# Feature-major sample columns, S5's a and final states transposed on TensorE instead of moved by element, and B loaded in two transfers

## The chip, the cores and the metric

The kernel runs on one core of a Trainium2 chip. The metric is the device time of one execution in microseconds; the figure for a kernel is the median of its runs. TensorE (PE) multiplies matrices, VectorE (DVE), ScalarE (ACT) and GpSimd (POOL) work element by element, and SyncE (SP) does nothing but issue transfers. ACT issues transfers too, on a queue of its own.

## What is computed

One inference step of a decoder of two layers, for a prompt of 2048 tokens and, beside it, 8 sample sequences of one token each. Both use the same weights.

```
for each layer l:
    proj = rms_norm(x) @ w_in[l]          # 1024 -> 3336 columns, cut into 15 groups
    A  retention on r_q, r_k, r_v         B  mLSTM on m_q, m_k, m_v, m_i, m_f
    C  S5 (complex diagonal SSM) on s_u   D  attention of a_q into 256 memory tokens
    mix = [A | B | C | D], each times its SiLU gate
    x   = x + mix @ w_out[l]
outputs: rms_norm(x) of prompt and sample, and each group's final states
```

The S5 group has 16 channel groups of 64 complex states: a (16x64, real and imaginary), B (16x64x16), C (16x16x64). Its final prompt states are outputs of 16x64 each. The state of the 8 samples is read from inputs, advanced by one token and written back.

## The kernel before

The prompt is cut into 4 units of 512 tokens a layer. A unit runs through the column groups of w_in in a fixed order (`ORDER`): m_v, s_u, then the four quarters of w_out for the unit before, m_k, m_q, m_o, a_q, r_k, r_v, r_q, s_g, a_g, m_g, r_g; in unit 1 of layer 0 the four quarters of w_out come after a_q. Weights are kept as two float32r halves. The first time that a group's weights are used they are loaded raw, split on ACT, DVE and POOL and stored to DRAM (`ws`); later units load both halves from there (`w<-ws`, 256 KB a transfer, on SP). Each product is three matmuls, high x high, high x low, low x high.

Seven groups (`FEAT`: m_k, m_q, a_q, s_g, a_g, s_u, r_q) are computed feature-major, features on partitions and tokens in columns; the others token-major. In unit 1 of each layer (the sample unit) the 8 sample tokens are computed as well. For a feature-major group they are 8 more columns behind the 512 of the prompt, and each of its two halves of 128 features is done in two pieces of 260 columns. The second piece ends in the 8 sample columns. Line 480 copies them out of PSUM, and line 481 stores them to the DRAM table `sproj[l]` (8 rows of 3336 columns), which lies sample-major: 128 partitions x 8 columns become 1024 runs of one element. That is 14 stores a layer. For token-major groups `sample_group` (from line 1538) multiplies the 8 samples by themselves and stores rows of 256 columns.

Work beside the main groups is written as generators that are stepped after every main step (`sides`, `step_sides`). `s5_pre` builds the S5 tables of a layer: layer 0's from the start, layer 1's, slowed by a factor, from unit 2 of layer 0 on. Its first step (lines 1121 to 1129) loads a with four transfers by element (partition = state, column = channel group, so 64x16 single elements each), dt, and B with four transfers of 1024 runs of 64 B (real over imaginary, and imaginary over real). `s_core` is the S5 of a unit: it loads tables by quarters (`s_tables`: sWi, sCS, sTW), runs a scan on DVE, carries the state in `xprev` (128 x 16), sends Y through DRAM to turn it and, in the last unit, stores `xprev` with two transfers of 1024 elements (lines 1390 to 1392). `sample_layer` starts after the sample unit's r_g, slowed as well; it reads `sproj` back in many layouts and ends in stores to `smix`, which the last unit's w_out groups need. Its S5 part, `sample_s5`, loads u, feature on partition, with eight transfers of 32 x 8 elements (lines 1784 and 1785).

`dma` issues on SP, `dmaa` on ACT. Small tiles come from rotating pools: `sm` has 17 buffers, `t1` 3, `t2` 12, and `bank()` gives one of four PSUM banks `ps`; a new tile waits until its buffer's last reader is done. The tile framework plans the order of the instructions of each engine when the program is built, from a simulated timeline; within an engine, and within a queue, the planned order is kept. Helpers record one line for all their callers: `mm` 181, `tr` 185, `act` 188, `dma` 191, `dmaa` 194.

Of the kernel before, what the change touches and what calls it, by code (L numbers as in the profile page):

```python
# [22 lines left out]
SG = 16  # L23
# [5 lines left out]
D_IN = 3336  # L29
# [4 lines left out]
NB = 8  # L34
# [80 lines left out]
def AP(t, off, ap):  # L115
    return bass.AP(tensor=t.tensor, offset=t.offset + off, ap=[list(x) for x in ap])


class Builder:
# [93 lines left out]
    def setup(self):  # L213
        nc, I, cp = self.nc, self.I, self.cp
        c = lambda n, s, dt=F32: cp.tile(s, dt, name=n, tag=n)
        self.ident = c("ident", [128, 128])
        self.dma(self.ident, I["c_ident"])
        self.wstream()
        self.mem_load()
        self.wload(0)  # L220
        self.hnl = self.hn_load(0, 0)
        next(self.hnl)
        self.wload(1)
        self.maskb = c("maskb", [128, 512], BF16)
        self.identb = c("identb", [128, 128], BF16)
        mt = self.t2([128, 512])
        self.dma(mt, I["c_mask"])
        nc.vector.tensor_copy(self.maskb, mt)
        nc.vector.tensor_copy(self.identb, self.ident)
        self.Dt = c("Dt", [128, 2, 2, 128])  # L230
        self.dma(self.Dt, I["c_D"])
        self.vd = c("vd", [128, H])
        self.dma(self.vd, I["c_vd"])
        self.ropes = c("ropes", [128, 2, 16])
        self.dma(self.ropes, I["c_ropes"])
        self.smc = c("smc", [128, 4])
        self.dma(self.smc, I["c_sm"])
        self.e127 = c("e127", [128, 1])
        self.dma(self.e127, I["c_e127"])
        self.s32 = c("s32", [128, 32])  # L240
        self.dma(self.s32, I["c_s32"])
        self.s8 = c("s8", [128, 8])
        self.dma(self.s8, I["c_s8"])
        st = self.t2([128, H])
        self.dma(st, I["c_sel"])
        self.sel = c("sel", [128, H], F32R)
        nc.vector.tensor_copy(self.sel, st)
        zero = self.t2([128, 320])
        nc.vector.memset(zero, 0.0)
        self.ones = c("ones", [128, 1])  # L250
        nc.vector.memset(self.ones, 1.0)

        self.hT = [cp.tile([128, 8, UT + NB], F32R, name=f"hT{i}", tag=f"hT{i}") for i in range(2)]
        self.Sr = [c(f"Sr{i}", [128, 2, 128]) for i in range(3)]
        self.Cm = [c(f"Cm{i}", [128, 2, 130]) for i in range(3)]
        for t in self.Sr + self.Cm:
            nc.vector.memset(t, 0.0)
        self.mprev = c("mprev", [4, 8])
        self.hS = [c(f"hS{i}", [128, 8, 40], F32R) for i in range(2)]
        for i in range(2):  # L260
            nc.vector.tensor_copy(self.hS[i].rearrange("p a b -> p (a b)"), zero)

        T = self.T
        self.xd = [self.dram([T, D], f"xd{i}") for i in range(self.depth)]
        self.xsd = [self.dram([NB, D], f"xsd{i}") for i in range(self.depth)]
        self.sproj = [self.dram([NB, D_IN], f"sproj{i}") for i in range(self.depth)]
        self.smix = [self.dram([NB, D], f"smix{i}") for i in range(self.depth)]
        self.stab = []
        self.memd = []
        for l in range(self.depth):  # L270
            self.stab.append(dict(
                Wi=self.dram([128, SG, 128], f"Wi{l}"), TW=self.dram([128, 3, 1024], f"TW{l}"),
                CS=self.dram([128, 2, SG, 128], f"CS{l}"), Kd=self.dram([32, 16, 112], f"Kd{l}"), ab=self.dram([128, 3, SG], f"ab{l}"),
                C1=self.dram([128, SG, SC], f"C1{l}")))
            self.memd.append((self.dram([128, 2, MEM], f"mk{l}"), self.dram([128, 2, GW], f"mv{l}")))
# [173 lines left out]
    def group(self, i):  # L449
        kind, l, b, g = self.wseq[i]  # L450
        if i == 0:
            self.wsplit(0, 0)
            self.wsplit(0, 1)
        hi, lo, _ = self.wspl[i]
        if kind == "mem":
            self.mem_group(l, b, hi, lo)
            self.advance(i, 0)
            self.advance(i, 1)
            yield
        elif kind == "out":  # L460
            if self.sample_in_unit(kind, l, b):
                while not self.smix_done[l]:
                    self.step_sides()
                self.sample_group(i, l, g, hi, lo, kind)
            yield from self.group_out(i, l, b, g, hi, lo)
        elif g in FEAT:
            if g == "r_q":
                for m in range(2):
                    self.u["rq", m] = self.g4([128, 2, UT], n="rqt")
                    self.dmaa(self.u["rq", m], self.I["c_rq"][b, m])  # L470
            smp = self.sample_in_unit(kind, l, b)
            pieces = [(0, 260), (260, 520)] if smp else [(0, UT)]
            for m in range(2):
                for c0, c1 in pieces:
                    ps = self.feat_bank(m, hi, lo, slice(c0, c1))
                    c2 = min(c1, UT)
                    self.evac_f(l, b, g, m, ps[:, :c2 - c0], slice(c0, c2))
                    if c1 > UT:
                        o = self.sm([128, 16])[:, :NB]
                        self.nc.vector.tensor_copy(o, ps[:, c2 - c0:c1 - c0])  # L480
                        self.dma(AP(self.sproj[l], COL[g] + 128 * m, [[1, 128], [D_IN, NB]]), o)
                    if (c0, m) == (0, 0):
                        self.advance(i, 0)
                    if c1 >= UT and m == 1:
                        self.advance(i, 1)
                    yield
        else:
            if g == "m_v":
                jobs = [[t] for t in range(4)]
            else:  # L490
                jobs = [[0, 1], [2, 3]]
            n = 264 if g == "m_v" else 256
            for m, ts in enumerate(jobs):
                sls = [slice(t * 128, (t + 1) * 128) for t in ts]
                ps = self.tok_bank(sls, n, hi, lo, self.hslice)
                self.evac(l, b, g, m, ps)
                if m in (0, len(jobs) - 1):
                    self.advance(i, min(m, 1))
                if g == "r_g":
                    nxt = self.next_unit(l, b)  # L500
                    if nxt:
                        self.hn_T(2 * m)
                        self.hn_T(2 * m + 1)
                yield
        if kind == "in" and g not in FEAT and self.sample_in_unit(kind, l, b):
            self.sample_group(i, l, g, hi, lo, kind)
# [605 lines left out]
    def s5_pre(self, l):  # L1112
# [5 lines left out]
        packA = self.t2([128, 512], n="packA")  # L1118
        packC = self.t2([128, 2, SG, SC], n="packC")
        ar, ai, dt = S(), S(), S()  # L1120
        for h in range(2):
            self.dma(ar[64 * h:64 * h + 64], I["s5_a_re"][l].rearrange("g p -> p g"))
            self.dma(ai[64 * h:64 * h + 64], I["s5_a_im"][l].rearrange("g p -> p g"))
        self.dma(dt, AP(I["s5_log_dt"][l], 0, [[0, 128], [1, SG]]))
        Bst = P1([2, SG, SC], "Bst")
        for h in range(2):
            for w in range(2):
                src = I["s5_b_re" if h == w else "s5_b_im"][l]
                self.dma(Bst[64 * h:64 * h + 64, w], src.rearrange("g p c -> p g c"))
        yield  # L1130
        yield
        self.pexp(dt, SG)
        mag, th, cs, sn, k, tmp, thl = S(), S(), S(), S(), S(), S(), S()
        v.tensor_tensor(mag, ar, dt, OP.mult)
# [186 lines left out]
    def s_core(self, u, l, b):  # L1321
# [66 lines left out]
        yield  # L1388
        yield
        if b == self.NU - 1:  # L1390
            for h, on in enumerate(("s5re_p", "s5im_p")):
                self.dma(self.O[on][l, 0].rearrange("g p -> p g"), self.xprev[64 * h:64 * h + 64])
        gl = self.g4([128, 2, UT], n="gl")
        gh_, gl_ = [self.g4([128, 2, UT], F32R, n="gls") for _ in range(2)]
        for gh in range(2):
# [142 lines left out]
    def sample_group(self, i, l, g, hi, lo, kind):  # L1538
# [16 lines left out]
        else:  # L1555
# [5 lines left out]
            if g == 3:  # L1561
                if l + 1 < self.depth:
                    self.dma(self.xsd[l], self.xrow)
                    self.sample_hn(l + 1, self.xrow)
                else:
                    w = self.bcrow(self.I["final_norm_w"])
                    self.rms_rows([self.xrow], w[:NB], NB)
                    self.dma(self.O["y_sample"].rearrange("b o d -> (b o) d"), self.xrow)

    def s_load(self, t, l, name, width, off=0, outer=True):  # L1570

# [201 lines left out]
    def sample_s5(self, l, lc):  # L1773
# [8 lines left out]

        uT = self.s64([128, 8, NB], n="suT")
        for pr in range(8):
            self.dma(uT[96:128, pr, :], AP(dr, COL["s_u"] + 32 * pr, [[1, 32], [D_IN, NB]]))
        st = self.t1([128, 2, 128], n="sst")
        for w, nme in enumerate(("state_s5_re", "state_s5_im")):
            src = I[nme][l].rearrange("b g p -> (b g) p")
# [201 lines left out]
```

## Time and profile before

| | |
|---|---|
| Median of 3 runs | 2325.03 us (2319.82 to 2328.70) |
| Profiled execution | 2328.93 us, span 2327.1 us |
| PE busy | 2160.1 us, 93% of the span |
| DVE, ACT, POOL busy | 61%, 33%, 17% |
| Mean granted clock of TensorE | 0.962 |
| DMA packets | 392905, of these 115800 under 512 B |

The chain that ended last is PE for the most part of what it names, mainly the matmuls of the column groups (`pm`, line 181); DMA has 6% of it, weight loads first. Times below count from the start of the span. A unit is taken to end where line 540 has copied the last piece of the next unit's m_v: at 69.3, 295.4, 624.1, 890.0 and 1180.4 us in layer 0 and at 1442.0, 1747.6 and 2009.2 in layer 1. The sample units are 295.4 to 624.1 and 1442.0 to 1747.6. Busy times of PE are modelled at their ends, so they are a little high.

### The profile page before, as it was taken

How to read it: one execution, taken by the hardware profiler on the slowest of the kernel's cores; microseconds unless marked ns; L12 is line 12 of the kernel's file. 1: busy time of each engine (PE TensorE's matmuls, PEld its weight loads, DVE VectorE, ACT ScalarE, POOL GpSimd, SP SyncE). 2: the span in 40 equal slices, each digit the busy share in tenths (PEclk: the TensorE clock that was granted, in tenths of full speed). 3: DMA queues.
4: the chain of work that ended last, by engine and by line, in shares of the span. 5: the costliest groups of instructions: out<-in, count | busy, mean ns of one | idle time of the engine just before them, and what ended most of it. 6: DMA issues, size and time to landing. Idle time of an engine off the chain costs nothing. (4 is left out here: it accounts for less than half of the span.)

```text
span 2327.1 us, 44458 instructions
## 1 busy us (share of the span) xinstructions
PE 2160.1 (93%) x16386; PEld 1991.0 (86%) x16386; DVE 1424.2 (61%) x3883; ACT 778.3 (33%) x1842; POOL 405.5 (17%) x435
## 2 busy tenths in 40 slices
PE   7889977899999999989899999898999899999998
PEld 6688967899997888888798989887899788888888
DVE  7787855535465687565944768355465466656463
ACT  4445422323223332134422454222331233312332
POOL 3343111111001113120202331110100001121011
PEclk9999988999999999989999999898999999999999
DMA  7878587978686656877568884996877776598634
GB/s 223 297 251 270 201 163 140 225 257 139 175 276 202 219 187 214 294 146 230 160 199 281 267 275 149 242 287 132 176 142 258 273 222 209 185 315 211 180 116 153
DMA packets 392905, 496.88 MB, mean 214 GB/s; under 512 B 115800, under 2 KB 216344, under 8 KB 392688
## 3 DMA queue, kind: packets, MB, share of 16 engines
q1 hardware_dynamic: 366848, 433.61, 64.3%
q10 hardware_dynamic: 25840, 60.43, 8.8%
q8 instruction: 129, 2.11, 0.4%
q14 instruction: 88, 0.72, 0.1%
HBM read 376.75 MB, written 118.21 MB: 213 GB/s over the span
## 5 line engine op out<-in xcount | busy, mean ns | idle before, releaser
L181 PE MATMUL pm<-hT,w 128*128 128x512 f32 (+1 forms) x3360 | 681.4, 358 | 9.2 <-ACT w L188 5.9
L181 PEld LDWEIGHTS pm<-hT,w 128*128 128x128 f32 x3360 | 550.7, 193 | 98.1 <-ACT w L188 6.5
L181 PE MATMUL pm<-w,hT 128*128 128x256 f32 (+1 forms) x4608 | 607.8, 288 | 12.8 <-DMA w<-ws 5.0
L181 PEld LDWEIGHTS pm<-w,hT 128*128 128x128 f32 x4608 | 574.1, 193 | 21.4 <-DMA w<-ws 7.2
L181 PE MATMUL pm<-w,mix 128*128 128x256 f32 x3072 | 379.8, 285 | 3.7 <-ACT w L188 2.1
L181 PEld LDWEIGHTS pm<-w,mix 128*128 128x128 f32 x3072 | 372.8, 192 | 4.9 <-ACT w L188 2.3
L366 POOL TENSOR_TENSOR w<-w,w 128x512 fp32r<-128x512 f32 (+1 forms) x76 | 110.0, 1448 | 370.4 <-ACT w L188 158.9
L188 ACT ACTIVATE w<-w 128x512 fp32r<-128x512 f32 (+1 forms) x152 | 95.0, 633 | 181.2 <-DMA w<-w_in 78.1
L1358 POOL TENSOR_TENSOR sA<-sy,sCS 128x512 f32<-128x512 f32 x32 | 53.0, 1658 | 363.1 <-DVE sy L1355 162.0
L366 DVE TENSOR_TENSOR w<-w,w 128x512 fp32r<-128x512 f32 (+1 forms) x76 | 54.6, 720 | 87.7 <-ACT w L188 73.2
L188 ACT ACTIVATE Pt<-ps,sm 128x256 f32<-128x256 f32 x128 | 58.9, 472 | 114.5 <-DVE sm L994 93.0
L1454 DVE TENSOR_TENSOR xr<-xr,pm 128x512 f32<-128x512 f32 x56 | 38.2, 684 | 78.2 <-PE pm L181 32.4
L188 ACT ACTIVATE sB<-ps 64x512 f32<-64x512 f32 x64 | 37.9, 592 | 107.9 <-DVE sy L1347 83.7
L1355 DVE TENSOR_TENSOR_SCAN sy<-ab,xprev,sy 128x128 f32<-128x128 f32 x128 | 57.3, 505 | 0.6
L1414 POOL TENSOR_TENSOR t<-t,s_g 128x512 f32<-128x512 f32 x16 | 25.4, 1584 | 175.2 <-DVE t L1412 83.7
L643 POOL TENSOR_TENSOR r_k<-rp 128x256 f32<-128x256 f32 x32 | 24.2, 759 | 181.8 <-DVE rp L641 160.3
L993 DVE TENSOR_REDUCE sm<-ps 128x2 f32<-128x512 f32 x64 | 42.3, 685 | 21.2 <-PE ps L181 20.9
L181 PE MATMUL ps<-X,sWi 128*128 128x128 f32 x256 | 38.6, 297 | 17.2 <-DMA sWi<-Wi 11.2
L588 POOL TENSOR_TENSOR r_qT<-rqs,rqs 128x512 f32<-128x512 f32 (+2 forms) x20 | 22.0, 1100 | 184.5 <-DVE rqs L587 100.3
L898 POOL TENSOR_TENSOR vw<-mv,RT 128x260 f32<-128x260 f32 x32 | 22.1, 699 | 178.5 <-DVE sm L1109 69.4
L181 PEld LDWEIGHTS ps<-X,sWi 128*128 128x128 f32 x256 | 33.1, 202 | 21.6 <-issue 21.5
L185 PE MATMUL ps<-ident,xt 128*128 128x128 f32 x256 | 38.2, 300 | 13.2 <-DVE xt L387 11.5
(434 smaller groups left out, 3308.5 us busy)
## 6 DMA issues: line engine op xcount, KB each, us to landing
w<-ws SPq DMA_DIRECT2D x768, 256.0 KB
ws<-w SPq DMA_DIRECT2D x256, 256.0 KB
w<-w_in SPq DMA_DIRECT2D x104, 256.0 KB
sCS<-CS SPq DMA_DIRECT2D x32, 512.0 KB
xd<-xr SPq DMA_DIRECT2D x56, 256.0 KB
w<-ws SPq DMA_DIRECT2D x48, 264.0 KB
sTW<-TW SPq DMA_DIRECT2D x32, 384.0 KB
xt<-x_prompt ACTq DMA_DIRECT2D x16, 512.0 KB
```

What stands on the lines that cost most here:

```text
L181: self.nc.tensor.matmul(out, lhsT, rhs, start=start, stop=stop, skip_group_check=skip)
L185: self.nc.tensor.transpose(out, in_, self.ident[:K, :K])
L188: self.nc.scalar.activation(out, in_, f, **kw)
L366: e.tensor_tensor(lo[q], r[q], hi[q].bitcast(F32), OP.subtract)
L588: self.nc.gpsimd.tensor_tensor(u["r_qT"][:, m, c], q, qs, OP.add)
L643: gp.tensor_tensor(dst[:, x, :], t1.rearrange("p h f -> p (h f)"), t2.rearrange("p h w f -> p (h w f)"), OP.add)
L898: gp.tensor_tensor(vw, mv[:, j], RT[:, j, 3, :, None].to_broadcast([128, H, 65]), OP.mult)
L993: v.tensor_reduce(mx[:, 2 * x:2 * x + 2], ps[x].rearrange("p (a m) -> p a m", a=2), AX.X, OP.max)
L1355: v.tensor_tensor_scan(t1[:, g], self.abt[:, 2, gg:gg + 1].to_broadcast([128, 128]), t1[:, g], self.xprev[:, gg:gg + 1], OP.mult, OP.add)
L1358: gp.tensor_tensor(A[:, :, 1:129], t1, Cs, OP.mult)
L1414: gp.tensor_tensor(zg.rearrange("p (j s) -> p j s", s=4), z.rearrange("p (s j) -> p j s", s=4), u["s_g", m].rearrange("p (j s) -> p j s", ...
L1454: v.tensor_tensor(xr, xr, ps.rearrange("p (t c) -> p t c", t=2), OP.add)
```

## The change

The 14 pieces of sample columns of a layer are gathered in one SBUF tile `sft` (128 features x 14 pieces x 8 samples). When the last is in, a side step `sample_feat` transposes it once on PE, copies the result (112 rows of 128) out of PSUM on ACT and stores it with seven transfers whose rows are 128 columns long. `sample_s5` takes u from `sft` by ACT copies. `s5_pre` loads a in its own layout (rows of 64), transposes it on PE and copies it out on DVE; of B it loads one order and copies the other on ACT. `s_core` transposes `xprev` before it stores the final states by rows of 64.

```diff
--- before.py
+++ after.py
@@ -266,6 +266,7 @@
         self.sproj = [self.dram([NB, D_IN], f"sproj{i}") for i in range(self.depth)]
         self.smix = [self.dram([NB, D], f"smix{i}") for i in range(self.depth)]
         self.stab = []
+        self.sft = {}
         self.memd = []
         for l in range(self.depth):
             self.stab.append(dict(
@@ -476,9 +477,13 @@
                     c2 = min(c1, UT)
                     self.evac_f(l, b, g, m, ps[:, :c2 - c0], slice(c0, c2))
                     if c1 > UT:
-                        o = self.sm([128, 16])[:, :NB]
-                        self.nc.vector.tensor_copy(o, ps[:, c2 - c0:c1 - c0])
-                        self.dma(AP(self.sproj[l], COL[g] + 128 * m, [[1, 128], [D_IN, NB]]), o)
+                        if "sft" not in self.u:
+                            self.u["sft"] = self.tb([128, 2 * len(FEAT), NB], "sft")
+                            self.u["sft_n"] = 0
+                        self.nc.vector.tensor_copy(self.u["sft"][:, 2 * FEAT.index(g) + m, :], ps[:, c2 - c0:c1 - c0])
+                        self.u["sft_n"] += 1
+                        if self.u["sft_n"] == 2 * len(FEAT):
+                            self.sides.append(self.sample_feat(l, self.u["sft"]))
                     if (c0, m) == (0, 0):
                         self.advance(i, 0)
                     if c1 >= UT and m == 1:
@@ -1118,17 +1123,23 @@
         packA = self.t2([128, 512], n="packA")
         packC = self.t2([128, 2, SG, SC], n="packC")
         ar, ai, dt = S(), S(), S()
-        for h in range(2):
-            self.dma(ar[64 * h:64 * h + 64], I["s5_a_re"][l].rearrange("g p -> p g"))
-            self.dma(ai[64 * h:64 * h + 64], I["s5_a_im"][l].rearrange("g p -> p g"))
+        at = P1([2, 128], "at")[:SG]
+        for w, nme in enumerate(("s5_a_re", "s5_a_im")):
+            for h in range(2):
+                self.dma(at[:, w, 64 * h:64 * h + 64], I[nme][l])
         self.dma(dt, AP(I["s5_log_dt"][l], 0, [[0, 128], [1, SG]]))
         Bst = P1([2, SG, SC], "Bst")
         for h in range(2):
-            for w in range(2):
-                src = I["s5_b_re" if h == w else "s5_b_im"][l]
-                self.dma(Bst[64 * h:64 * h + 64, w], src.rearrange("g p c -> p g c"))
-        yield
-        yield
+            self.dma(Bst[64 * h:64 * h + 64, 0], I[("s5_b_re", "s5_b_im")[h]][l].rearrange("g p c -> p g c"))
+        yield
+        yield
+        ps = self.bank()
+        for w in range(2):
+            self.tr(ps[:, SG * w:SG * w + SG], at[:, w])
+        v.tensor_copy(ar, ps[:, 0:SG])
+        v.tensor_copy(ai, ps[:, SG:2 * SG])
+        for h in range(2):
+            self.act(Bst[64 * h:64 * h + 64, 1], Bst[64 - 64 * h:128 - 64 * h, 0])
         self.pexp(dt, SG)
         mag, th, cs, sn, k, tmp, thl = S(), S(), S(), S(), S(), S(), S()
         v.tensor_tensor(mag, ar, dt, OP.mult)
@@ -1388,8 +1399,12 @@
         yield
         yield
         if b == self.NU - 1:
+            ps = self.bank()
+            self.tr(ps[:SG, :128], self.xprev)
+            xo = self.t1([128, 128], n="xo")[:SG]
+            self.act(xo, ps[:SG, :128])
             for h, on in enumerate(("s5re_p", "s5im_p")):
-                self.dma(self.O[on][l, 0].rearrange("g p -> p g"), self.xprev[64 * h:64 * h + 64])
+                self.dma(self.O[on][l, 0], xo[:, 64 * h:64 * h + 64])
         gl = self.g4([128, 2, UT], n="gl")
         gh_, gl_ = [self.g4([128, 2, UT], F32R, n="gls") for _ in range(2)]
         for gh in range(2):
@@ -1567,6 +1582,18 @@
                     self.rms_rows([self.xrow], w[:NB], NB)
                     self.dma(self.O["y_sample"].rearrange("b o d -> (b o) d"), self.xrow)
 
+    def sample_feat(self, l, sft):
+
+        self.sft[l] = sft
+        yield
+        n = 2 * len(FEAT) * NB
+        ps = self.bank()
+        self.tr(ps[:n, :128], sft.rearrange("p g b -> p (g b)"))
+        o = self.t1([128, 264], n="sfo")
+        self.act(o[:n, :128], ps[:n, :128])
+        for i, g in enumerate(FEAT):
+            self.dma(AP(self.sproj[l], COL[g], [[128, 2], [D_IN, NB], [1, 128]]), o[2 * NB * i:2 * NB * (i + 1), :128])
+
     def s_load(self, t, l, name, width, off=0, outer=True):
 
 
@@ -1782,7 +1809,7 @@
 
         uT = self.s64([128, 8, NB], n="suT")
         for pr in range(8):
-            self.dma(uT[96:128, pr, :], AP(dr, COL["s_u"] + 32 * pr, [[1, 32], [D_IN, NB]]))
+            self.act(uT[96:128, pr, :], self.sft[l][32 * (pr % 4):32 * (pr % 4) + 32, 2 * FEAT.index("s_u") + pr // 4, :])
         st = self.t1([128, 2, 128], n="sst")
         for w, nme in enumerate(("state_s5_re", "state_s5_im")):
             src = I[nme][l].rearrange("b g p -> (b g) p")
```

## Rows read from the trace of the kernel before

**Rows 1.** Page, engines: busy us, share of the span, instructions.

```profile
PE 2160.1 (93%) x16386; PEld 1991.0 (86%) x16386; DVE 1424.2 (61%) x3883; ACT 778.3 (33%) x1842; POOL 405.5 (17%) x435
```

**Rows 2.** Windows by unit: length, busy us (count) by engine, PEclk, DMA share, GB/s.

```profile
295.40:624.10 328.70, 288.43 (x2361) 277.86 (x2360) 165.10 (x415) 98.54 (x247) 46.88 (x45) 0.92 0.81 182
624.10:890.00 265.90, 256.94 (x1897) 232.51 (x1896) 176.41 (x565) 85.77 (x207) 32.36 (x44) 0.99 0.67 213
1180.40:1442.00 261.60, 256.24 (x1939) 234.97 (x1938) 158.21 (x389) 98.97 (x228) 53.25 (x48) 0.99 0.74 242
1442.00:1747.60 305.60, 274.69 (x2282) 266.03 (x2281) 158.73 (x436) 94.60 (x235) 39.34 (x41) 0.93 0.84 196
1747.60:2009.20 261.60, 253.66 (x1881) 230.20 (x1880) 158.01 (x462) 78.58 (x197) 24.25 (x25) 0.99 0.69 227
```

**Rows 3.** Groups: operation, tiles, shapes, count | busy us, mean ns | idle before.

```profile
L181 PE MATMUL ps<-w,hS 128*40 128x256 f32 (+1 forms) x320 | 41.4, 281 | 0.0
L185 PE MATMUL ps<-ident,xt 128*128 128x128 f32 x256 | 38.2, 300 | 13.2 <-DVE xt L387 11.5 <-DVE hT L420 1.0 <-DVE sm L203 0.4
L188 ACT ACTIVATE cso<-ps 64x256 f32<-64x256 f32 x2 | 0.8, 377 | 9.9 <-PE ps L185 9.9
```

**Rows 4.** DMA issues by tiles: queue, count, KB each.

```profile
sproj<-sm SPq DMA_DIRECT2D x28, 4.0 KB
sm<-s_a_re SPq DMA_DIRECT2D x4, 4.0 KB
suT<-sproj SPq DMA_DIRECT2D x16, 1.0 KB
```

**Rows 5.** Windows of 10 us, columns as in group 2.

```profile
310.00:320.00 10.00, 9.15 (x77) 8.95 (x75) 6.04 (x22) 4.68 (x12) 0.00 (x0) 1.00 0.86 76
1565.00:1575.00 10.00, 10.00 (x81) 9.65 (x80) 4.20 (x11) 1.53 (x5) 0.62 (x1) 0.86 0.65 16
```

**Rows 6.** Timeline of SP's queue: start, us to issue, transfer, count.

```profile
1561.61 2.35 SPq L191 DMA_DIRECT2D sproj<-sm  x2
1564.05 6.09 SPq L191 DMA_DIRECT2D sCS<-CS  x1
```

**Rows 7.** Chain of work that ended last: start us, us, what.

```profile
1570.87 13.40 DMA sTW<-TW
...
2126.74 12.08 DMA w<-ws
```

**Rows 8.** PE's waits, first and second sample unit: total us, times, longest.

```profile
PE ps L181 <- DVE sm L862: 7.4, 1, 7.4
PE ps L181 <- DMA sWi<-Wi: 6.6, 1, 6.6
...
PE ps L181 <- DMA sproj<-sm: 6.0, 1, 6.0
PE ps L181 <- DVE E L904: 5.2, 1, 5.2
...
PE ps L181 <- issue: 13.4, 2, 8.9
PE ps L185 <- ACT rows L188: 7.4, 1, 7.4
```

**Rows 9.** Timeline of SP's queue from 580 us.

```profile
586.83 0.93 SPq L191 DMA_DIRECT2D sproj<-sm  x1
587.98 3.23 SPq L191 DMA_DIRECT2D sm<-s_a_im  x1
...
608.37 0.78 SPq L191 DMA_DIRECT2D sq<-sproj  x1
```

**Rows 10.** Timeline of SP's queue at the final states.

```profile
2114.21 0.75 SPq L191 DMA_DIRECT2D s5im_p<-xprev  x1
...
2119.69 7.38 SPq L191 DMA_DIRECT2D w<-ws  x2
```

**Rows 11.** One window behind these stores, columns as in group 2.

```profile
2109.00:2160.00 51.00, 48.48 (x335) 43.49 (x336) 33.99 (x93) 12.99 (x44) 10.28 (x10) 0.90 0.79 144
```

## Prediction

> **What bounds the kernel now.** The profiled execution took 2328.93 us (span 2327.1, so 1.8 us lie around it); the median of the three runs is 2325.03, 3.9 us under it. I make the sum against the profiled execution and take 3.9 off at the end. A measurement of this kernel tells about 0.5% (11.6 us) from no change.
>
> I read the page's busy times first: TensorE (PE) is busy for 93% of the span [rows 1]. So nothing that is taken off another engine counts unless it closes a gap on PE or keeps PE's clock up, and all gaps together are 167 us. Then I cut the span into the kernel's units (one pass of 512 tokens through one layer), at the moments when the m_v group of the next unit is done, and read each stretch for PE's busy time and its granted clock [rows 2]. What a unit loses is its length less PE's busy time, plus its length times what the clock lacks of 1.00. That second term is a little high, since part of the slow clock falls into the gaps.
>
> Three units without sample columns and without a change of layer lose 8.96 + 2.7 = 11.6, 5.36 + 2.6 = 8.0 and 7.94 + 2.6 = 10.6 us, 10.1 on average. The two units that carry the sample columns lose 40.3 + 0.08 x 328.7 = 66.6 and 30.9 + 0.07 x 305.6 = 52.3 us. They lose 56.5 + 42.2 = 98.7 us more than the quiet ones do. Their lengths say it more carefully: 328.7 + 305.6 - 2 x 263.0 (the mean length of the quiet ones) = 108.3 us. Of these, the sample groups' own matmuls are some 16.6 us a unit (128 of the 320 in the row of 41.4 us [rows 3]), which leaves 75. So 75 to 99 us are what could be had in these two units. The question is how much of it the element transfers cause.
>
> The DMA side gives the answer's direction. In the quiet units a full DMA share stands for 213 / 0.67 = 318 to 329 GB/s; in the sample units for 182 / 0.81 = 225 and 196 / 0.84 = 233 [rows 2]. At 325 GB/s the sample units' bytes need shares of 0.56 and 0.60; the rest, 0.25 x 328.7 + 0.24 x 305.6 = 155 us, is DMA time that moves almost nothing. The transfers by element there are the 28 stores of sample columns [rows 4] and, in the first, layer 1's 4 loads of a and 4 of B; a 4 KB store is 1024 runs of one element. 155 / 36 is 4.3 us of all 16 DMA engines for each.
>
> Single places show it. Between 310 and 320 us the DMA engines are busy for 0.86 and move 76 GB/s, between 1565 and 1575 for 0.65 and move 16 GB/s [rows 5]. Each follows column stores: at 1561.61 two are issued, and then the next instruction on SP's queue, an S5 table load that has nothing to do with samples, takes 6.09 us to issue instead of some 0.5 [rows 6]. The chain of waits runs through that, through 13.40 us for the next table (sTW) to land, and on into a PE gap of 8.9 us [rows 7, 8].
>
> **The change part by part.** *Sample columns.* 28 stores of 1024 elements go; 14 stores of 16 rows of 512 B come, after all 14 pieces of a layer are in, with 2 PE transposes and 2 ACT copies. The 28 DVE copies only change their target. To price the removal I take PE's waits in the two units, one by one, and keep those that end on a table or weight load, or on an engine held by one, within some 15 us after a column store. These are 7.4 (DVE sm, behind an ACT queue that waited for U to reach DRAM), 6.6, 6.0 and 5.2 us in layer 0, and 7.4 (ACT rows) and 13.4 us (issue) in layer 1 [rows 8]: 46.0 of 71.2 us of gaps, 65%. If the clock loss goes with its gaps, that is 0.65 x 75 to 0.65 x 99, 49 to 64 us. I take 50, the lower end, because a load that is no longer late uncovers the next one. The bounds are 0 (all of it would be late anyway) and 99.
>
> The stores now come in a burst. In layer 0 the last column store is issued at 586.83 and the first load that reads the columns back at 608.37 [rows 9], so a transpose, a copy and seven issues have 20 us. Queued behind the burst on SP are weight loads (w<-ws); the seven carry 56 KB, a fifth of one 256 KB weight tile. On ACT the copy out of PSUM stands behind the transpose, and the evacuations of m_g and r_g behind it. I charge nothing; if the burst were as slow as seven old stores it would cost 7 x 4.3 = 30 us of DMA time in one place, and of that at most the 8.9 us gap.
>
> *S5's a and B.* Per layer 4 loads of 1024 elements [rows 4] become 4 loads of 16 rows of 256 B, with two PE transposes and two DVE copies; 2 of 4 B loads (1024 runs of 64 B each) become ACT copies of 64x256. Layer 1's loads lie at 586 to 608, in the sample unit, and are within its 50 us: they are issued beside a column store, and the second a load takes 3.23 us to issue [rows 9]. Layer 0's lie in the first 60 us; PE lacks at most a few us there and I put 1 us, bounds -5 (PE stands at a transpose for loads that only DVE waited for before) and 5.
>
> *Final states.* Two stores of 1024 elements a layer become a transpose, an ACT copy and two stores of 16 rows. In layer 1 the second is issued at 2114.21, and the two weight loads issued from 2119.69 take 7.38 us on SP [rows 10]; a weight load then lands 12.08 us late on the chain [rows 7], and the 51 us from 2109 lose 2.5 us of gaps and 0.10 x 51 = 5.1 us of clock [rows 11]. That is 7.6, of which a quiet stretch would keep some 2: gain 5. In layer 0 the gaps around them come before the stores are issued; gain 0.
>
> *The sample's u (uT).* 8 loads of 256 elements a layer [rows 4] become 8 ACT copies of 32x8. Both lie beside full PE stretches and the sample chain; gain 0, and they spare SP 16 issues.
>
> *What it adds.* Transposes: 4 a layer, 8 in all, at most 0.3 us each [rows 3]: 2.4 us on PE, charged at 2. ACT copies: 4 of B, 4 from PSUM, 16 of uT, at no more than the 0.377 us of a 64x256 copy [rows 3]: 9 us on an engine that is busy for 33% [rows 1]; hidden. If they were not, they would cost those 9 us. Each transpose waits on PE's in-order queue for its operand and for one of four PSUM banks, with all matmuls queued behind it; no row shows these waits. The nearest are PE's waits for ps, 5.2 to 8.9 us [rows 8]; the copies they wait for are done long before in the program's order, so I take 0 and keep the other end as a rival.
>
> **Sum:** 50 + 1 + 5 - 2 = 54 us. 2328.9 - 54 = 2275 us, and by the median 2271.
>
> **Rivals.**
> *The stretch is slow for other reasons.* The sample units also split each feature group in two pieces, store w_out's halves for the first time in each layer and evacuate more on DVE and ACT; then the same loads are late without the column stores. For it: quiet units have waits for sWi and for weights too. Against it: 16 GB/s at 0.65 share just after two such stores, and 155 us of DMA time without bytes. It gives the 1 + 5 us and little else: 2319. [...]
> *Half.* The loads come on time, but S5's scan chain on DVE, which runs through both units, becomes late instead: 25 us, 2300.
> *All of it.* The sample units become quiet units: 75 to 99 us and the rest, about 85 + 4: 2236, at the most 2222.
> *Slower.* The new transposes hold PE. There are six groups of them (a, columns, states, in two layers). If each stood as long as PE's longest wait for ps, 8.9 us, and the clock took its share besides (in the sample units 47.7 us of clock to 71.2 us of gaps, two thirds), that is 6 x 8.9 x 1.67 = 89 us against 54 gained: 2325 + 35 = 2360. It decides from 54 / 6 = 9 us a group, wait and clock together; below that the change stays ahead. Against it: the operands are there early (a's loads two steps before, xprev before Y goes through DRAM and back, the columns one step before).
>
> **How the numbers follow.** Forecast (gain 35 to 75) 0.57, half 0.15, all of it 0.12, slow for other reasons 0.10, slower 0.06. Faster by over 0.5%: 0.57 + 0.15 + 0.12 = 0.84; within 0.5%: 0.10; slower: 0.06. The range leaves out the slower case and a part of the two that border on it: 2225 to 2320, low end from nearly the whole excess, high end from the rival that gains 6 us.
>
> **What would show it.** Right: in the stretches of the two sample units the DMA share falls to about 0.6 at the same bytes or the rate rises to over 210 GB/s, both units come to about 300 and 285 us, issues of SP after a feature group stay under 2 us, and the run's packets fall by about 48 700 (45 056 of one element and 4096 of B go, some 420 come). Wrong: these fall and PE's gaps stay, with other releasers; or the longest PE waits are on the transposes of at, sft and xprev; or a load of sproj by the sample layer becomes late.

## The result and the profile after

The median went from 2326.75 us (four runs now) to 2229.3 us, a ratio of 0.957 with a 95% interval of 0.9535 to 0.9612. One of the four runs of the changed kernel took 2313.76 us at a granted clock of 0.845, against 0.979 to 0.984 in the others, and the ratio leaves it out. The gain is 97 us where 54 were forecast, inside the range and near the rival "all of it". The profiled execution took 2230.52 us (span 2228.7), 98.4 us less than that of before.

The page of the kernel after, engines and packets:

```profile
PE 2130.2 (96%) x16394; PEld 1965.2 (88%) x16394; DVE 1428.4 (64%) x3887; ACT 784.7 (35%) x1866; POOL 400.2 (18%) x435
...
DMA packets 343430, 496.61 MB, mean 223 GB/s; under 512 B 66100, under 2 KB 166868, under 8 KB 343212
```

PE's gaps fell from 167 to 98.5 us [rows 1]. Packets fell by 49 475 (some 48 700 were expected), nearly all of them under 512 B, at nearly the same bytes (496.88 MB before). The five units of [rows 2], cut at the same instruction in the kernel after (columns as there):

```profile
296.30:573.00 276.70, 271.59 (x2362) 263.45 (x2362) 165.53 (x415) 100.22 (x250) 46.62 (x45) 0.99 0.66 216
573.00:844.60 271.60, 261.79 (x1907) 236.40 (x1906) 181.47 (x571) 87.02 (x209) 33.99 (x46) 0.97 0.66 211
...
1127.70:1391.30 263.60, 257.93 (x1936) 236.43 (x1935) 159.03 (x388) 98.96 (x228) 53.42 (x48) 0.99 0.75 241
1391.30:1654.10 262.80, 260.94 (x2284) 254.47 (x2282) 159.74 (x436) 94.33 (x236) 41.02 (x41) 1.00 0.68 229
1654.10:1914.80 260.70, 254.11 (x1881) 230.16 (x1880) 157.61 (x462) 78.55 (x197) 23.95 (x25) 0.99 0.69 226
```

The two sample units are 52.0 and 42.8 us shorter, 94.8 of the 98.4. Their matmuls are as many as before within two (2362 and 2284), but the gaps went from 40.3 and 30.9 us to 5.1 and 1.9, and the clock from 0.92 and 0.93 to 0.99 and 1.00. A full DMA share now stands for 327 and 337 GB/s in them, as in the quiet units; the 155 us of DMA time without bytes are gone. All other units together came to 3.6 us less (single ones moved by up to 7.3 us, either way).

PE's waits in the first and the second sample unit, all that are listed (total us, times, longest), against [rows 8]:

```profile
PE ps L181 <- DMA X<-ud: 3.8, 1, 3.8
PE ps L181 <- DVE Cm L926: 1.0, 1, 1.0
PE ps L185 <- DVE if L807: 0.3, 1, 0.3
...
PE ps L185 <- ACT rows L188: 1.0, 1, 1.0
PE ps L181 <- DMA sWi<-Wi: 0.8, 1, 0.8
```

No transpose of at, sft or xprev is among them. SP's queue in the kernel after, first around the two halves of U, then at the burst of stores (start us, us to issue, transfer, count):

```profile
311.12 2.96 SPq L191 DMA_DIRECT2D w<-ws  x6
...
530.68 0.38 SPq L191 DMA_DIRECT2D sm<-s_log_dt  x1
539.16 4.46 SPq L191 DMA_DIRECT2D sproj<-sfo  x7
543.73 3.74 SPq L191 DMA_DIRECT2D w<-ws  x8
...
552.66 0.74 SPq L191 DMA_DIRECT2D sq<-sproj  x1
```

The six weight loads that follow the first U take 2.96 us. In the kernel before the same six, with one column store ahead of them, took three times as long:

```profile
310.21 8.96 SPq L191 DMA_DIRECT2D w<-ws  x6
```

SP now stands for 8.1 us before the seven new stores (until the copy out of PSUM is done), with eight weight loads behind them; PE waited for none. The reader comes 13.5 us after the first of the seven.

### The profile page after: what moved, and what is told of

Read it like the earlier page. It is cut to its first block, busy times and chain, and to the rows that moved or that the text cites. A ratio compares the mean times of both kernels' runs of the same rounds, so it can differ in the third digit from the quotient of the medians.

```text
span 2228.7 us, 44433 instructions
## 1 busy us (share of the span) xinstructions
PE 2130.2 (96%) x16394; PEld 1965.2 (88%) x16394; DVE 1428.4 (64%) x3887; ACT 784.7 (35%) x1866; POOL 400.2 (18%) x435
## 5 line engine op out<-in xcount | busy, mean ns | idle before, releaser
L181 PE MATMUL pm<-w,hT 128*128 128x256 f32 (+1 forms) x4608 | 598.2, 286 | 6.7 <-ACT hT L188 3.1
L181 PEld LDWEIGHTS pm<-w,hT 128*128 128x128 f32 x4608 | 565.2, 190 | 14.0 <-ACT hT L188 5.5
L181 PE MATMUL pm<-w,mix 128*128 128x256 f32 x3072 | 373.1, 282 | 0.6 <-ACT mix L188 0.6
L181 PEld LDWEIGHTS pm<-w,mix 128*128 128x128 f32 x3072 | 366.3, 189 | 1.2 <-ACT mix L188 0.8
L188 ACT ACTIVATE w<-w 128x512 fp32r<-128x512 f32 (+1 forms) x152 | 94.8, 633 | 145.0 <-DMA w<-w_in 55.3
L1358 DVE TENSOR_TENSOR sy<-ps,sCS 128x512 f32<-128x512 f32 x32 | 22.1, 690 | 38.1 <-PE ps L181 35.7
```

Of the source, the lines that this page charges most:

```text
L181: self.nc.tensor.matmul(out, lhsT, rhs, start=start, stop=stop, skip_group_check=skip)
L188: self.nc.scalar.activation(out, in_, f, **kw)
L1358: v.tensor_tensor(t1, p3, Cs, OP.mult)
```

## The experiments

Three theories were set against each other at first: A, the column stores by element cost all of it; B, every transfer by element costs by its number of runs; C, the new plan of the order made the gain. Kernels that are compared below ran on the same chip beside the kernel before, whose median was 2322.43 us on the chip of the first four, 2368.12 on that of the second four and 2350.77 on that of the last four. Where two runs come from different chips, compare their ratios and not their times.

### One part alone

```diff
 # the kernel before, plus only:
+ sft gathered, sample_feat stores it in rows of 128 columns
```

> Of the change, the sample columns alone: gathered in SBUF, transposed once, stored in rows of 128 columns. a, B, the final states and the sample's u stay transfers by element. Theory A (the 28 column stores by element caused the two sample units' whole loss): those two units keep 276 and 263 us, except that layer 1's a and B loads (8 transfers of 1024 runs) come back into the end of the first one and cost 4.3 us each of DMA time, so some 10 us; in all 2235 to 2250 us. Theory B (all transfers by element matter alike, by their number of runs): the columns are 28 672 of 49 152 runs, 58%, so 0.58 x 98 = 57 us are gained: 2270 us. Theory C (the new plan of the instructions' order made the gain): no relation, anywhere between 2229 and 2325.

Measured: 2231.99 us, ratio 0.9587 (0.9527 to 0.9646). The two sample units:

```profile
293.00:570.50 277.50, 272.36 (x2362) 264.28 (x2360) 163.14 (x416) 99.25 (x248) 46.54 (x45) 0.99 0.68 216
...
1384.60:1646.90 262.30, 261.11 (x2284) 254.66 (x2282) 158.84 (x437) 94.68 (x236) 40.99 (x41) 1.00 0.68 229
```

They are those of the whole change, although layer 1's loads of a and B by element still lie in the first. So these loads cost nothing that the time shows, and theory B is out: 58% of the runs gave all of the gain.

```diff
 # the kernel after, with
-self.nc.vector.tensor_copy(self.u["sft"][...], ps[...])  # and sample_feat, uT from sft
+o = self.sm([128, 16])[:, :NB]; ...; self.dma(AP(self.sproj[l], ..., [[1, 128], [D_IN, NB]]), o)
```

> The counterpart: a, B and the final states as changed, the 28 column stores by element and the sample's u by element back. Theory A: only the tail's 4 us, the start's 4 us and the a and B loads' share in the first sample unit are gained: 2305 to 2320 us. Theory B: 12 288 of 49 152 runs go, 25%, 24 us: 2302 us. If the gains of this and of the columns alone add up to 98 us, the parts act by themselves; if they fall short, the parts relieve the same place only together.

Measured: 2329.5 us, ratio 1.0026 (0.9995 to 1.0057): a, B and the final states without the columns gave nothing. Its sample units keep the loss:

```profile
293.20:612.30 319.10, 285.48 (x2361) 274.07 (x2360) 164.70 (x416) 99.45 (x249) 47.28 (x45) 0.93 0.81 188
...
1435.40:1741.20 305.80, 273.05 (x2282) 263.73 (x2281) 160.23 (x436) 94.53 (x235) 39.64 (x41) 0.94 0.86 197
```

### The store put back beside the change

From here on the changed kernel does its work as it is, and each of the 28 pieces is also stored into DRAM that nobody reads. Only the target's addresses, or the width of a value, change from one to the next.

```diff
 self.u["sft_n"] += 1
+self.dma(AP(self.scr[l], ..., [[1, 128], [128, NB]]), self.u["sft"][:, 2 * FEAT.index(g) + m, :])
```

> The changed kernel, and besides it each of the 28 pieces of sample columns is also stored by element (1024 runs of 4 B, from the same tile, at the old moment) into DRAM that nobody reads. Theory A (the stores themselves cost it): the two sample units grow by about 95 us again, 2315 to 2330 us in all, with DMA share about 0.82 at 185 to 200 GB/s in them. Theory C (order, pools, or where the readers wait): only the issues come back, 28 x 0.4 us on a queue with slack; 2229 to 2240 us.

Measured: 2330.1 us, ratio 1.0022 (0.9992 to 1.0051). Stores whose data nobody needs bring the whole loss back, so it lies in none of the readers:

```profile
296.60:625.00 328.40, 285.32 (x2362) 275.55 (x2360) 164.45 (x415) 100.19 (x250) 46.87 (x45) 0.92 0.77 182
...
1440.10:1751.20 311.10, 275.27 (x2284) 265.79 (x2282) 159.59 (x437) 94.66 (x236) 40.01 (x41) 0.93 0.79 193
```

PE's longest waits in the first of them are in the main the kinds of [rows 8] again:

```profile
PE ps L181 <- DVE PT L1024: 10.5, 1, 10.5
PE ps L181 <- DMA scr<-sft: 9.7, 1, 9.7
PE ps L181 <- DMA sWi<-Wi: 7.7, 1, 7.7
PE ps L181 <- DVE E L911: 6.7, 1, 6.7
```

The first, PT of the attention, I had left out of my list in the kernel before (6.0 us there) because I could tie it to no column store.

```diff
+self.dma(AP(self.scr[l], ..., [[NB, 128], [1, NB]]), self.u["sft"][:, 2 * FEAT.index(g) + m, :])
```

> The same 28 extra stores at the same moments with the same 4 KB each, but laid out so that each partition's 8 values are one run: 128 runs of 32 B in place of 1024 of 4 B. Theory A, cost by the number of runs: an eighth of what the extra stores of 1024 runs cost, about 12 us: 2235 to 2245 us. If a transfer costs by being there (issue, semaphore, its write's receipt): the same as with 1024 runs, 2315 us or more.

Measured: 2232.16 us, ratio 0.9592 (0.9544 to 0.9641). The same bytes at the same moments in 128 runs of 32 B are free, even of the 12 us that theory A gave them. Between the two stores lie 97.9 us, 3.5 us a store.

### Number of runs, or their neighbours

1024 against 128 runs left two readings: the number of runs, or the 4 B that each writes. Four kernels took these apart, with the queue and the direction.

```diff
+wide = self.s64([128, NB, 8], n="wide")   # each value eight times, by one more DVE copy
+self.dma(AP(self.scr[l], ..., [[8, 128], [1024, NB], [1, 8]]), wide)
```

> The changed kernel, and 28 extra stores at the old moments of 1024 runs of 32 B each (each value eight times, 32 KB a store) into DRAM that nobody reads. If the number of runs is what is paid: as with 1024 runs of 4 B, 2315 to 2335 us. If the size of the single write is what is paid (4 B being the bad case): near the 2232 us of 128 runs of 32 B, up to 2245 us for eight times the bytes.

Measured: 2238.46 us, ratio 0.9432 (0.94 to 0.9464).

```diff
+self.dma(AP(self.scr[l], 0, [[1024, 128], [128, NB], [1, 1]]), self.u["sft"][...])   # all pieces of a layer to the same addresses
```

> The same extra stores of 1024 runs of 4 B, but each partition's eight values lie 512 B apart and the partitions 4096 B apart, so that no two runs of a store fall into the same 512 B. If runs are paid by their number: 2315 to 2335 us again. If the cost came from neighbouring values that are merged into one block of DRAM by different engines: well below, 2235 to 2270 us.

Measured: 2239.18 us, ratio 0.9441 (0.9412 to 0.9469). So 1024 runs are free when each is 32 B, and 1024 runs of 4 B are free when they lie 512 B apart. Packets agree with those of the dear store, the share does not; the page's packets and the first sample unit of the run with runs apart:

```profile
DMA packets 372549, 496.72 MB, mean 222 GB/s; under 512 B 95220, under 2 KB 195988, under 8 KB 372332
...
299.10:575.60 276.50, 271.44 (x2361) 262.83 (x2360) 164.54 (x415) 100.08 (x250) 46.95 (x45) 0.99 0.71 217
```

and the packets of the run with neighbouring runs:

```profile
DMA packets 372549, 496.72 MB, mean 213 GB/s; under 512 B 95220, under 2 KB 195988, under 8 KB 372332
```

The number of runs is out as the cause. What is left is that 4 B writes fall close to one another.

```diff
+xl = self.sm([128, 16], n="xl")
+self.dma(xl[:, :NB], AP(self.I["w_in"][l], ..., [[1, 128], [D_IN, NB]]))   # a load by element, and a small DVE copy
```

> The changed kernel, and 28 extra loads of 1024 elements (4 B each from w_in) into small tiles, free to go early. Runs paid by their number whichever way they go: 2315 to 2335 us. If only stores by element are dear, as a and B's lack of effect in the run without column changes suggests: 2230 to 2250 us.

Measured: 2240.11 us, ratio 0.9436 (0.9398 to 0.9473). The same pattern of addresses, read instead of written, is free, though all 28 loads are issued within the two sample units.

```diff
 # the kernel before, with
-self.dma(AP(self.sproj[l], COL[g] + 128 * m, [[1, 128], [D_IN, NB]]), o)
+self.dmaa(AP(self.sproj[l], COL[g] + 128 * m, [[1, 128], [D_IN, NB]]), o)
```

> The kernel before, with the 28 column stores by element issued from ACT's queue and everything else as it was. Theory A1 (the runs fill SP's queue, so that what is issued behind them on SP is late): the weight and table loads go past them, most of the gain comes: 2235 to 2270 us. Theory A2 (the runs occupy the 16 DMA engines themselves, whatever the queue): 2310 to 2330 us, the same loss with the loads late on the engines instead of at the issue.

Measured: 2367.44 us, ratio 0.9994 (0.9967 to 1.0021): the same loss from another queue. The first store from ACT's queue, and what SP then does (two timelines):

```profile
304.74 0.39 ACTq L194 DMA_DIRECT2D sproj<-sm  x1
...
308.38 0.34 SPq L191 DMA_DIRECT2D sWi<-Wi  x1
308.81 10.14 SPq L191 DMA_DIRECT2D w<-ws  x6
```

SP needs 10.14 us for the six weight loads although no store stands in its own queue. So SP's slow issues are a result: its transfers meet the stores somewhere behind the queues. This run doesn't show where.

### How close is close

```diff
+self.dma(AP(self.scr[l], ..., [[8, 128], [1024, NB], [1, 1]]), self.u["sft"][...])    # 32 B apart
```

> The changed kernel, and 28 extra stores of 1024 runs of 4 B at the addresses of the runs of 32 B: neighbouring partitions are 32 B apart, 16 of them in 512 B. Stores 4 B apart cost some 95 to 130 us, stores 512 B apart nothing. If what is paid is that runs share the same 32 B: as 512 B apart, 2230 to 2245 us. If they pay for sharing one block of 512 B: 2300 us or more.

Measured: 2235.02 us, ratio 0.95 (0.9472 to 0.9528). This kernel has the same instructions in the same order on every engine as the dear one of 2330.1 us; they differ by the addresses of the dead stores alone. The two ran on different chips, but against the kernel before on its own chip the dear one comes to 1.0022 and this one to 0.95. Theory C, the plan, is out with that. SP's rows behind the first store, here and then in the dear one:

```profile
309.70 0.39 SPq L191 DMA_DIRECT2D scr<-sft  x1
...
313.24 3.40 SPq L191 DMA_DIRECT2D w<-ws  x6
```

```profile
307.82 0.39 SPq L191 DMA_DIRECT2D scr<-sft  x1
...
311.35 9.81 SPq L191 DMA_DIRECT2D w<-ws  x6
```

3.40 against 9.81 us for the same six loads. Windows at the same distance from that first store's issue, some 4 to 12 us behind it, show what the loads meet (here, then in the dear one; columns as in [rows 2]):

```profile
314.00:322.00 8.00, 8.00 (x69) 7.98 (x68) 6.47 (x22) 5.06 (x12) 1.23 (x1) 1.00 0.98 284
```

```profile
312.00:320.00 8.00, 8.00 (x69) 8.00 (x68) 3.57 (x12) 2.78 (x7) 0.00 (x0) 1.00 0.77 44
```

In both kernels the store's own packets have gone by then: in the packed traces over 95% of them start within 4 us of the issue, and the median one takes 9 ns here and there. What is slow in the dear kernel is what comes behind them, 44 GB/s in place of 284.

```diff
+self.dma(AP(self.scr[l], ..., [[16, 128], [2, NB], [1, 1]]), self.u["sft"][...])    # a partition's 8 values 8 B apart
```

> The same with each partition's 8 values 8 B apart in 64 B of its own, so that eight partitions in a row share 512 B and no 64 B hold values of two partitions. If the cost comes from values of different partitions (which come by different engines) that meet in one small block: 2230 to 2245 us. If any 4 B writes close to one another cost it, one partition's own too: 2300 us or more.

Measured: 2308.27 us, ratio 0.9815 (0.9784 to 0.9846), 73.3 us over the runs 32 B apart on the same chip, 2.6 us a store. These two also have the same instructions in the same order. No two partitions share 64 B here, and it is dear all the same; so it is not values of different partitions that must meet. That they cost more where they do meet is possible and not shown: the kernel before lies 115.8 us over the runs 32 B apart on this chip. The dear patterns put 8 or more writes of 4 B into 64 B, the free ones two at most. Which block it is that counts (16, 32 or 64 B), and whether what follows the store is held up in the DMA engines or at the memory, stays open.

### The parts that gave little or nothing

```diff
 # the kernel after, with
-self.dma(at[:, w, 64 * h:64 * h + 64], I[nme][l])    # tr, copies, B's ACT copies
+self.dma(ar[64 * h:64 * h + 64], I["s5_a_re"][l].rearrange("g p -> p g"))    # and four B loads
```

> The changed kernel with a and B loaded as before (8 loads of 1024 elements, 8 of B). Loads by element cost nothing in their own test, and the changed a and B put 16 small instructions and a wait into the start: if so 2224 to 2232 us, the same or a few us less than the change, with the first two units some 3 us shorter (the run with the columns alone has them at 293.0 us, the change at 296.3). If runs of loads do matter in the first sample unit: 2235 to 2245 us.

Measured: 2233.24 us, ratio 0.9495 (0.9468 to 0.9521). The first two units take 296.3 us in both kernels. So loading a and B by element costs nothing here. The medians of the change and of this run (2229.3, 2233.24) come from different chips, so neither is shown to be the better one.

```diff
 # the kernel after, with
-self.tr(ps[:SG, :128], self.xprev); ...; self.dma(self.O[on][l, 0], xo[:, 64 * h:64 * h + 64])
+self.dma(self.O[on][l, 0].rearrange("g p -> p g"), self.xprev[64 * h:64 * h + 64])
```

> The changed kernel with the four final-state stores by element back (1024 runs of 4 B, 16 rows of 64 neighbouring values each). If neighbouring 4 B writes are what is dear, four of them cost up to 4 x 3.4 us of DMA time; those of layer 1, in the last unit, show with up to 7 us there: 2232 to 2240 us. If the last unit hides them: 2226 to 2232 us.

Measured: 2234.85 us, ratio 0.9495 (0.947 to 0.952). The 51 us around its two stores of layer 1, cut as [rows 11] (from 4.5 us before the first of them), then the same stretch of the work in the kernel after, which has no store by element there (each begins some 4 us before the last write of `xprev`):

```profile
2012.00:2063.00 51.00, 44.97 (x323) 39.41 (x323) 34.93 (x94) 13.11 (x44) 8.33 (x9) 0.93 0.88 152
```

```profile
2011.00:2062.00 51.00, 49.77 (x401) 45.79 (x400) 41.70 (x108) 16.47 (x53) 9.49 (x10) 1.00 0.63 177
```

With the stores by element the stretch loses 6.0 us of gaps and 3.6 of clock, with the change 1.2 of gaps and nothing of clock. These stores put 64 neighbouring values of 4 B into a row, so they are of the dear kind, and they act like it: a high DMA share at a low rate. What follows gives about half of that back. The 51 us behind it, with the stores by element and then with the change, and in the change DVE's row and PE's wait there:

```profile
2059.00:2110.00 51.00, 50.15 (x309) 43.41 (x308) 25.28 (x66) 18.45 (x49) 4.42 (x4) 0.97 0.68 186
```

```profile
2059.00:2110.00 51.00, 47.89 (x257) 39.26 (x256) 16.46 (x44) 14.98 (x34) 2.58 (x2) 0.93 0.56 188
...
2068.75 0.39 DVE L971 COPY cst<-Cm 64x64 f32<-64x64 f32 x2 [6.27 <-DMA s5im_p<-xo]
...
PE ps L185 <- DVE cst L971: 3.1, 1, 3.1
```

The change's copy of the states, `xo`, takes one of the three `t1` buffers until its stores have landed; the copy of the mLSTM state (`cst`) waits for a buffer on DVE, and PE for that copy. This stretch loses 6.7 us with the change and 2.4 with the stores by element, which have no `xo`. The last unit takes 319.7 us with the states by element, 313.9 with the change and 315.3 with a and B back, but it spreads from 313.9 to 323.4 over the ten kernels here that have the new state stores (mean 317.9), and from 317.9 to 328.5 over the four with the old ones (mean 323.0). The medians of this run and of the one with a and B back lie only 1.6 us apart on the same chip.

## Why the prediction was right, and where its sizes were off

**What bounds it: right.** The loss sat almost wholly in the two sample units: 94.8 of 98.4 us, and the run with the columns alone gives all of it.

**The bound of 75 to 99 us: the upper end was true, the lower one too low.** I took the sample groups' matmuls (16.6 us a unit) off as work that stays. They stayed, but the sample units are now about as long as the quiet ones: 276.7 and 262.8 us against a mean of 265.3 for the three quiet units. They lose 7.9 and 1.9 us by the measure of the prediction (gaps and clock), the quiet ones 8.3 to 18. By that measure the two fell from 118.9 to 9.8 us, 14 more than they got shorter; the prediction had said that it is a little high. A unit's loss is not a base that every unit pays.

**"I take 50": the mis-sized term.** It measured 94.8. Two choices made it small. I kept 46.0 of 71.2 us of gaps, those that I could tie to a column store; 7.0 us are left, so those that I could not tie (PT, Sr, the weight splits) went with the stores as well; the run with the dead stores brings PT (10.5 us) and Sr (2.6 us) back. By which way they hang on the stores was not followed. And I went to the lower end because a load that is no longer late "uncovers the next one"; the waits that are left are 3.8 us at most. The clock followed the gaps as assumed. That the time still lies in the range is owed to the range's width: its low end, 2225, allowed for nearly the whole excess.

**The price of a transfer: right in total, wrong in its cause.** 155 us of DMA time were spread over 36 transfers by their number of runs. Loads of a and B have no part in it, so it is 5.5 us for each of the 28 stores. And the number of runs is not what is paid: 1024 runs of 4 B that lie 32 or 512 B apart cost nothing. The issue of 6.09 us [rows 6] was real, but it came from how close the writes lie. Nor is it the time of the stores' own packets: it is that of the transfers behind them, which moved 44 GB/s in place of 284.

The Trainium skill (DMA: Bandwidth & Descriptors, "Specifications") says that transfers under 512 B are read, modified and written. Here writes of 4 and of 32 B that share 512 B with others show no cost in time (2235.02, 2238.46 us) as long as no more than two of them fall into 64 B, so that figure doesn't tell where the cost of these stores begins.

**The burst: right at nothing.** Seven stores took 4.46 us to issue, and no wait of PE follows.

**a and B: right at about nothing.** A gain of 1 us was forecast for layer 0; the first two units went from 295.4 to 296.3 us. That layer 1's loads were "within its 50" was wrong: alone they matter nothing.

**Final states: right where they were priced, half lost behind.** Forecast was a gain of 5 us in the 51 us around the stores of layer 1. That stretch lost 7.6 us and now loses 1.2. But the change loses 4.3 us more than the stores by element in the stretch behind, and over the whole kernel the gain is not shown: the last unit is 4.0 us shorter in the profiles of before and after, but the medians of the runs with the states back and with a and B back lie only 1.6 us apart, and a, B and the states alone gave nothing (2329.5 us).

**What it adds: the work right, one wait missing.** Transposes and copies in the kernel after (count, duration min/median/max ns, first and last start):

```profile
L185 PE MATMUL ps<-ident,at x4: 207/218/229, 54.9 to 590.2; 16*128 16x16 f32 x4
...
L185 PE MATMUL ps<-ident,sft x2: 272/272/273, 538.6 to 1620.1; 128*112 128x128 f32 x2
L188 ACT ACTIVATE suT<-sft x16: 204/206/207, 892.2 to 1954.6; 32x8 f32<-32x8 f32 x16
```

All are under the 0.3 and 0.377 us that were taken as upper bounds. The waits were taken as 0. No transpose waits for its own operand for long, but the buffer of `xo` makes PE wait 3.1 us for another one, that of `cst`.

**The rivals.** "Slow for other reasons" fell: dead stores alone bring the loss back. "Slower" fell: PE waits for none of the new transposes, and the 3.1 us behind `xo` are far from the 9 us a group at which it would have decided. "All of it" is what happened; it had 0.12.

## What to carry to other kernels

A store that scatters neighbouring 4 B values can hold up every other transfer of the core for several us while its own bytes are nothing; look for stretches where the DMA share is high and the rate low, and ask which store lies just before. Turn such data on TensorE, or lay the target out so that a run is 32 B, or that values lie 32 B apart; all three were free here, and it does not help to issue the store from another queue. When waits of many kinds crowd into one stretch, count the whole loss of the stretch against its neighbours rather than only the waits that can be tied to a cause. And look at what a new tile takes from a rotating pool: a tile that is stored holds its buffer until the store has landed.

## What was not expected of the hardware

- 28 stores of 1024 runs of 4 B: 2330.1 us with the runs side by side, 2308.27 with 8 B between a partition's values, 2235.02 with 32 B, 2239.18 with 512 B (1.0022, 0.9815, 0.95 and 0.9441 of the kernel before on the same chips). The change itself, without such stores, is 2229.3 (0.957).
- 28 loads of the same pattern: 2240.11 us.
- A crowded store's own packets are short (median 9 ns); for some 8 us behind them the DMA engines moved 44 GB/s at a share of 0.77, where they moved 284 behind a store with values 32 B apart.
- The kernel with the dear stores differs from chip to chip: the kernel before measured 2322.43, 2350.77 and 2368.12 us on three chips, kernels without column stores of that kind 2232 to 2240 on the same three.
